# Attention's modulation chunks in two buffers of their own: a two-layer hybrid decoder on one core

## The chip, the core and the metric

The kernel runs on one core of one Trainium2 chip. The metric is the device time of one execution in microseconds (us), as the median of several runs. The engines are named as the profile names them: PE (TensorE, matrix products), PEld (its weight loads), DVE (VectorE), ACT (ScalarE), POOL (GpSimd) and SP (SyncE, which issues nearly all the DMAs here).

## The reference

Two layers over 256 tokens of width 1024. Layer 0 mixes tokens with dilated sliding-window attention (three groups of 16 heads), layer 1 with gated linear attention; each is followed by a gated convolutional feed-forward block. Before every block stands an RMS norm whose scale and shift, like the gate of the residual, come from the conditioning vector:

```
for i in range(DEPTH):
    mod = silu(c) @ w_ada[i] + b_ada[i]            # 1024 -> 6 * 1024
    sh1, sc1, g1, sh2, sc2, g2 = split(mod, 6)
    h = rmsnorm(x, norm_mix[i]) * (1 + sc1) + sh1
    y = dilated_mixture(h, ...) if i % 2 == 0 else gla_mixer(h, ...)
    x = x + g1 * y
    h = rmsnorm(x, norm_ffn[i]) * (1 + sc2) + sh2
    x = x + g2 * conv_ffn(h, ...)
return rmsnorm(x, norm_final)
```

All of it is float32. The matrix `w_ada` is 48 MB in all, and serves a single vector.

## The kernel before

**Weights.** A weight piece is loaded by one DMA from SP into a tile `raw` of the pool `wraw` (four buffers of 2048 columns, 1 MB each over the 128 partitions). `split` (L162) then makes two halves of it for products in three passes: ACT copies `raw` to `whi` (L172, rounded), DVE subtracts to get `wlo` (L178, or L184 through `low_part`). `whi` and `wlo` have three buffers each. `mm3` (L196) multiplies hi by hi, hi by lo and lo by hi, all on PE.

**Modulation.** The product with `w_ada` is not done on PE. It comes in 48 chunks of 1 MB, two halves `s` of 1024 columns each. `ada_load` (L129) brings a chunk in, into the same four buffers of `wraw`; `ada_dot` (L136) multiplies a half with the broadcast `c_bc` and sums along the row in one DVE instruction (L140), then ACT adds the bias (L148 or L150). The first eight chunks are used by the start, one for each of eight blocks `kt` of the input. The other forty are taken one by one by `next_ada` (L441): two after the second attention unit, one after each of the three query-key groups of units 2 to 7 (20 in attention in all), the rest later. In a unit from 2 on, the dot products of a chunk are put behind the group's last evacuation on DVE (`behind(evacuate(...))`, L590); the load of the chunk is not, since `behind` orders only instructions of the same engine as the one named. The two chunks of unit 1 (L606) are behind nothing. In this text the chunks of attention are called c0, c1, c2 and so on; c0 and c1 are those of unit 1.

**Start.** For each `kt` there is a modulation chunk and a weight piece `w0[kt]` (1920 columns), both in `wraw`. The order of the start on DVE and ACT is written out by hand: two dots, the scaling of `x`, a half of `wlo`, `hlo`, the other half of `wlo`. PE multiplies the piece for units 0 and 1 at once (L571, L575).

**Attention.** Eight units (pairs of heads). A unit needs three query-key pieces `wqk` and two value pieces `wv`; a unit's scores and softmax (`attend`, L449) run beside the next unit's projections. Its tiles lie in the pool `att`, which ends with the output projection (`project`, L629). The last quarter of the output projection's weights goes into two tiles `w30` and `w31` of `att`, 1536 columns each, by `last_out` (L613), so that they don't take a place in `wspl`. No other instruction uses these two places.

**Order.** A list scheduler sets the order of each engine's queue: it runs a model of the machine, and whenever an engine is free it takes, of the instructions whose inputs and buffers are there, the one that is earliest in the program. `tc.issue_after` and `behind` add an edge that keeps an instruction behind another on its engine. The bias loads of attention, for example, are kept behind the last load of the start in this way:

```
with tc.issue_after(last_load[0].ins):
    bias = load_bias(u)
```

`shift(pool, columns)` puts an unused tile in a pool, to move what follows it.

Of the kernel before, what the change touches and what calls it, by code (L numbers as in the profile page):

```python
# [11 lines left out]
F32 = mybir.dt.float32  # L12
EXP_LN = "natural_log_exp_and_others"
F32R = mybir.dt.float32r
# [4 lines left out]
P = 128  # L19
D = 1024  # L20
# [37 lines left out]
def trunk(ctx: ExitStack, tc: tile.TileContext, I, out):  # L58
    nc = tc.nc
# [12 lines left out]
    def bank(name="ps", tag=None):  # L72
        tag = tag or next(cycle)
        return psum.tile([P, 512], F32, tag=tag, name=name, bufs={"p": 2, "s": 3, "t": 3}[tag])
# [24 lines left out]
    def col(at):  # L99
        return small[:, at : at + 1]  # L100
# [25 lines left out]

    mod = {}

    def ada_load(l, n, dmas=1):  # L129
        raw = wraw.tile([P, 2048], F32, tag="raw", name="ada_raw")  # L130
        for i in range(dmas):
            c = slice(2048 * i // dmas, 2048 * (i + 1) // dmas)
            nc.sync.dma_start(raw[:, c], I["w_ada"][l, n][:, c])
        return raw

    def ada_dot(l, n, s, raw):  # L136
        piece, kt = ADA_ORDER[2 * n + s]
        dot = tmp.tile([P, 1], F32, tag="dot", name="dot", bufs=4)
        w = raw[:, D * s : D * s + D]
        i = nc.vector.tensor_tensor_reduce(  # L140
            w, w, c_bc, op0=ALU.mult, op1=ALU.add, scale=1.0, scalar=0.0, accum_out=dot,
        )
        m = state.tile([P, 1], F32, tag=f"mod{l}{piece}{kt}", name="mod")
        b = col(C_BADA + 48 * l + 8 * piece + kt)
        if piece in (1, 4):
            g = col((C_NMIX if piece == 1 else C_NFFN) + 8 * l + kt)
            b1 = (16 if piece == 4 else 0) + 8 * l + kt
            j = nc.scalar.activation(m, dot, AF.Identity, scale=g, bias=one_b[:, b1 : b1 + 1])  # L148
        else:
            j = nc.scalar.activation(m, dot, AF.Identity, bias=b)  # L150
        mod[l, piece, kt] = m
        return i, j

    def ada_chunk(l, n):
        raw = ada_load(l, n)
        for s in range(2):
            ada_dot(l, n, s, raw)
# [4 lines left out]
    def split(src, n, dmas=1, after=((), ()), late=(), low=(), lows=True):  # L162
        raw = wraw.tile([P, 2048], F32, tag="raw", name="raw")
        for i in range(dmas):
            c = slice(n * i // dmas, n * (i + 1) // dmas)
            last_load[0] = nc.sync.dma_start(raw[:, c], src[:, c])
        hi = wspl.tile([P, 2048], F32R, tag="whi", name="whi")
        lo = wspl.tile([P, 2048], F32R, tag="wlo", name="wlo")
        for i in range(0, n, n // 2):
            c = slice(i, i + n // 2)  # L170
            with behind(*after[i > 0]):
                copied[0] = nc.scalar.copy(hi[:, c], raw[:, c])  # L172
        if not lows:
            return hi, lo, raw, n // 2
        for i in range(0, n, n // 2):
            c = slice(i, i + n // 2)
            with behind(*(late if i else low)):
                last_lo[0] = nc.vector.tensor_tensor(lo[:, c], raw[:, c], hi[:, c].bitcast(F32), op=ALU.subtract)  # L178
        return hi, lo
# [16 lines left out]
    def mm3(ps, a, b, start, stop):  # L196


        mm(ps, a[0], b[0], start=start, stop=False)  # L199
        mm(ps, a[0], b[1], start=False, stop=False)  # L200
        return mm(ps, a[1], b[0], start=False, stop=stop)  # L201
# [39 lines left out]
    def shift(pool, columns):  # L241

        pad = pool.tile([P, columns], F32, tag=f"pad{len(pads)}", name="pad")
        pads.append(pad)
# [25 lines left out]
    @contextmanager  # L270
    def behind(*those):

        with ExitStack() as st:
            for i in those:
                st.enter_context(tc.issue_after(i.ins))
            yield
# [28 lines left out]
    def shift_columns(l, sub):  # L305
        with behind(*chain[7]):
            for kt in range(KT):
                nc.scalar.copy(early_x[kt][:, T : T + 1], mod[l, 3 * sub, kt])
# [4 lines left out]
    def scale(l, sub, kt):  # L313
        i = nc.scalar.mul(early_x[kt][:, 0:T], x[kt], mod[l, 3 * sub + 1, kt][:, 0:1])
        if kt == 5:
            sixth[:1] = [i]

    def load_early(src):
        early = wraw.tile([P, 2048], F32, tag="raw", name="raw")
        nc.sync.dma_start(early[:, 0 : KT * P], src[:, 0 : KT * P])  # L320
        return early
# [24 lines left out]
    def residual(l, sub, kt, ps):  # L346
        g = mod[l, 3 * sub + 2, kt]
        with behind(*(last_sum if kt == 7 or (l, sub, kt) == (0, 0, 6) else ())):
            i = last_x[kt // 7] = nc.vector.scalar_tensor_tensor(x[kt], ps, g[:, 0:1], x[kt], op0=ALU.mult, op1=ALU.add)
        if kt < 6:  # L350
            squared[1] = i

    def parts(w, at, n=P):
        return w[0][:, at : at + n], w[1][:, at : at + n]
# [5 lines left out]
    att = at_pool.__enter__()  # L360
# [72 lines left out]
    with tc.issue_after(last_load[0].ins):  # L433
        nc.sync.dma_start(x_all, I["xT"])
        nc.sync.dma_start(rows_d, rows)
        nc.sync.dma_start(small[:, C_CW:], I["small"][:, C_CW:])

    o_hi, o_lo = [], []
    rest = [(0, n) for n in range(8, 24)] + [(1, n) for n in range(24)]

    def next_ada():  # L441
        if rest:
            ada_chunk(*rest.pop(0))
# [104 lines left out]
    for u in range(NPAIR):  # L548
# [10 lines left out]
        if u == 0:  # L559
# [5 lines left out]
            for kt in range(KT):  # L565
                s, e = kt == 0, kt == KT - 1

                for a, b in ((0, 0), (1, 0), (0, 1)):
                    for i in range(2 * NG):
                        w = parts(w0[kt], P * i)  # L570
# [10 lines left out]
        else:  # L581
            for g in range(NG):
                w = split(I["wqk"][u - 2, g], 2048)
                pqk = bank("pqk", "p")
                pq, pk = pqk[:, :T], pqk[:, T:]
                for kt in range(KT):
                    s, e = kt == 0, kt == KT - 1
# [4 lines left out]
        if u > 0:  # L592
            pv = [bank("pv", "p") for _ in range(2)]
            for half in range(2):
                with behind(*chain[7]):
                    w = split(I["wv"][u - 1, half], 1536)
# [11 lines left out]
                next_ada()  # L608
    o = list(zip(o_hi, o_lo))

    KO = 6

    def last_out(src):  # L613


        raw = wraw.tile([P, 2048], F32, tag="raw", name="raw")
        nc.sync.dma_start(raw, src)
        n = 2 * P * KO
        own = [att.tile([P, n], F32R, tag=f"w3{s}", name=("whi", "wlo")[s], bufs=1)[:, :] for s in range(2)]
        split_into([(raw[:, i : i + n // 2], own[0][:, i : i + n // 2], own[1][:, i : i + n // 2]) for i in (0, n // 2)],  # L620
                   exps[-1:], (norms[-2:-1], turned[-3:-2]))
        rest = [wspl.tile([P, 2048], F32R, tag=("whi", "wlo")[s], name=("whi", "wlo")[s])[:, :] for s in range(2)]
        split_into([(raw[:, n:], rest[0][:, 0 : 2048 - n], rest[1][:, 0 : 2048 - n])])
        shared[:] = [y[:, 2048 - n :] for y in rest]
        return lambda kt, i: parts(own, 2 * P * kt + P * i) if kt < KO else parts(rest, 2 * P * (kt - KO) + P * i)

    shared = []

    def project(src, o, l, sub):  # L629

        ends = []
        shift_columns(l, 1)
        for n in range(4):
            if l == 0 and n == 3:
                tile_of = last_out(src[n])
            else:

                w = split(src[n], 2048, **(dict(after=(evacuated[:1], ()), low=evacuated[1:]) if n == l == 0 else {}))
                tile_of = lambda kt, i, w=w: parts(w, 2 * P * kt + P * i)
            ps = [bank("py", "ppst"[n])] * 2  # L640
            if n == 3:
                ps[1] = bank("py", "s")
            order = [(kt, i) for kt in range(KT) for i in range(2)]
            if n == 3:
                order.sort(key=lambda x: x[1])
            for kt, i in order:

                first = {(2, 2): last_t, (2, 4): last_po, (2, 5): ends[:1], (3, 0): ends[2:]} if l == 0 else {(2, 2): ends[:1]}
                with behind(*first.get((n, kt), ())):
                    e = mm3(ps[i][:, T * i : T * i + T], tile_of(kt, i), o[kt],  # L650
                            kt == 0 and (n == 3 or i == 0), kt == KT - 1 and (n == 3 or i == 1))
            ends.append(e)
            if n == 3:
                early = load_early(I["w_up"][l, 0])
            for i in range(2):
                residual(l, sub, 2 * n + i, ps[i][:, T * i : T * i + T])
                squared_now = add_square(2 * n + i, alone=(l, n, i) == (0, 3, 0))
                if (l, n) != (0, 3):
                    scale(l, 1, 2 * n + i)
            if (l, n) == (0, 3):  # L660

                with behind(squared_now):
                    for i in range(2):
                        scale(l, 1, 2 * n + i)
        return early

    shift(att, 8)
    early = project(I["w_out_a"], o, 0, 0)
    at_pool.__exit__(None, None, None)


# [169 lines left out]
    for n in range(4):  # L841
        with behind(*((), chain[5], chain[7], glr_copy)[n]):
            w = split(I["w_v_b"][n], 2048) if n else w_first
# [309 lines left out]
```

## Time and profile before

| what | value |
|---|---|
| median of 3 runs | 783.05 us (782.6 to 783.72) |
| the profiled execution's own time | 784.99 us |
| its span, first to last instruction | 783.2 us |
| PE busy | 770.9 us (98%) |
| DVE busy | 643.2 us (82%) |
| ACT busy | 479.9 us (61%) |
| moved by DMA | 184.72 MB, mean 236 GB/s |
| granted PE clock | 0.998 |

The span is shorter than the execution's own time by 1.8 us, which lie before the first and after the last instruction. In the rows a matrix product's end is modelled, so that a busy PE is not a PE at its peak. Start takes the first 54 us or so, attention and its output projection run to about 297 us, the first feed-forward block to about 476 us, the second layer takes the rest.

### The profile page before, as it was taken

The page shows a single profiled execution, that of the slowest core. Times are in us where ns is not written, and L with a number is a line of the kernel's source. Part 1 is how long each engine was busy: PE and PEld are TensorE (multiplying, and loading weights), DVE is VectorE, ACT ScalarE, POOL GpSimd, SP SyncE. Part 2 cuts the span into 40 slices and gives each one's busy share as a digit, 9 for nine tenths or more (in the row PEclk, how much of TensorE's full clock was granted, in tenths as well). Part 3 has the DMA queues.
Part 4 walks back from the last instruction along what each step waited for, and adds up shares of the span by engine and source line. Part 5 has one row for each costly group of instructions (what it writes and reads, how often), then busy time and mean ns, then how long its engine had stood idle before and what let it go on. Part 6 is the DMA issues. An engine that isn't in the chain of part 4 may idle for free.

```text
span 783.2 us, 15925 instructions
## 1 busy us (share of the span) xinstructions
PE 770.9 (98%) x6430; PEld 743.2 (95%) x6430; DVE 643.2 (82%) x1160; ACT 479.9 (61%) x937; POOL 13.9 (2%) x40
## 2 busy tenths in 40 slices
PE   8999999999999999999999999999999999999997
PEld 6999999999999999999999998898999999999997
DVE  6999988879778858999998877797567898899662
ACT  5476565555555657876766646655667866667552
POOL 1000000000000000000000100000010000000000
PEclk9999999999999999999999999999999999999999
DMA  9999677596784736776645984965445665555651
GB/s 349 397 338 363 211 290 286 180 328 203 255 299 164 282 128 232 267 264 228 245 166 195 323 310 177 360 227 203 141 146 186 236 215 179 199 197 196 211 205 54
DMA packets 32616, 184.72 MB, mean 236 GB/s; under 512 B 5852, under 2 KB 7388, under 8 KB 16286
## 3 DMA queue, kind: packets, MB, share of 16 engines
q1 hardware_dynamic: 32160, 183.26, 65.8%
q8 instruction: 50, 0.82, 0.4%
q10 hardware_dynamic: 382, 0.45, 0.2%
q14 instruction: 24, 0.20, 0.1%
HBM read 182.59 MB, written 1.10 MB: 235 GB/s over the span
## 4 chain that ended last, share of the span: by engine, by line
PE 84%; DVE 6%; DMA 6%; ACT 2%; issue 1%; ACTq 0%; DVEq 0%
PE pab L199 10%; PE pab L200 10%; PE pab L201 10%; PE pqk L199 4%; PE pqk L200 4%; PE pqk L201 4%; PE pv L199 4%; PE pv L200 4%; PE pv L201 3%; PE pd L201 3%; PE pd L199 3%; PE pd L200 3%; DVE wlo L178 3%; PE pqk L571 2%; PE py L199 2%; PE py L200 2%
## 5 line engine op out<-in xcount | busy, mean ns | idle before, releaser
L172 ACT CAST whi<-raw 128x1024 fp32r<-128x1024 f32 (+4 forms) x270 | 243.0, 946 | 127.8 <-PE pab L200 40.1
L178 DVE TENSOR_TENSOR wlo<-raw,whi 128x1024 fp32r<-128x1024 f32 (+3 forms) x254 | 270.2, 1093 | 52.2 <-ACT whi L172 51.4
L201 PE MATMUL pab<-hhi,wlo 128*128 128x256 f32 x672 | 184.7, 276 | 0.0
L200 PE MATMUL pab<-hlo,whi 128*128 128x256 f32 x672 | 184.7, 276 | 0.0
L199 PE MATMUL pab<-hhi,whi 128*128 128x256 f32 x672 | 183.2, 277 | 0.0
L140 DVE CUSTOM_DVE_ANT_0 ada_raw<-ada_raw,c_bc 128x1024 f32<-128x1024 f32 x96 | 113.5, 1218 | 16.7 <-DMA ada_raw<-in_w_ada 16.7
L200 PEld LDWEIGHTS pab<-hlo,whi 128*128 128x128 f32 x672 | 126.0, 188 | 0.2
L201 PEld LDWEIGHTS pab<-hhi,wlo 128*128 128x128 f32 x672 | 126.1, 188 | 0.0
L199 PEld LDWEIGHTS pab<-hhi,whi 128*128 128x128 f32 x672 | 125.1, 188 | 0.1
L199 PE MATMUL pqk<-hhi,whi 128*128 128x256 f32 x392 | 109.2, 283 | 0.0
L200 PE MATMUL pqk<-hlo,whi 128*128 128x256 f32 x392 | 108.4, 281 | 0.0
L201 PE MATMUL pqk<-hhi,wlo 128*128 128x256 f32 x392 | 107.8, 282 | 0.0
L201 PE MATMUL pd<-ghi,wlo 128*128 128x256 f32 x352 | 97.2, 276 | 0.5 <-DVE wlo L178 0.5
L200 PE MATMUL pd<-glo,whi 128*128 128x256 f32 x352 | 97.1, 276 | 0.0
L199 PE MATMUL pd<-ghi,whi 128*128 128x256 f32 x352 | 96.8, 276 | 0.0
L199 PEld LDWEIGHTS pqk<-hhi,whi 128*128 128x128 f32 x392 | 73.4, 188 | 0.7
L200 PEld LDWEIGHTS pqk<-hlo,whi 128*128 128x128 f32 x392 | 73.3, 188 | 0.3
L201 PEld LDWEIGHTS pqk<-hhi,wlo 128*128 128x128 f32 x392 | 72.7, 188 | 0.9 <-issue 0.7
L201 PEld LDWEIGHTS pd<-ghi,wlo 128*128 128x128 f32 x352 | 66.1, 188 | 0.7 <-DVE wlo L178 0.7
L200 PEld LDWEIGHTS pd<-glo,whi 128*128 128x128 f32 x352 | 66.1, 188 | 0.0
L199 PEld LDWEIGHTS pd<-ghi,whi 128*128 128x128 f32 x352 | 65.9, 188 | 0.0
L725 ACT ACTIVATE r<-pab,small 128x256 f32<-128x256 f32 x86 | 46.7, 559 | 15.5 <-DVE r L728 15.4
(216 smaller groups left out, 1369.5 us busy)
## 6 DMA issues: line engine op xcount, KB each, us to landing
ada_raw<-in_w_ada SPq DMA_DIRECT2D x47, 1024.0 KB, 6.4
raw<-in_w_up SPq DMA_DIRECT2D x42, 1024.0 KB, 4.9
raw<-in_w_down SPq DMA_DIRECT2D x32, 704.0 KB, 5.5
raw<-in_wqk SPq DMA_DIRECT2D x18, 1024.0 KB, 6.9
raw<-in_wv SPq DMA_DIRECT2D x14, 768.0 KB, 4.7
raw<-in_w SPq DMA_DIRECT2D x7, 960.0 KB, 6.1
raw<-in_w_out_a SPq DMA_DIRECT2D x4, 1024.0 KB, 6.3
raw<-in_w_v_b SPq DMA_DIRECT2D x4, 1024.0 KB, 7.3
```

Source lines behind the costliest of these rows:

```text
L140: i = nc.vector.tensor_tensor_reduce(w, w, c_bc, op0=ALU.mult, op1=ALU.add, scale=1.0, scalar=0.0, accum_out=dot,)
L172: copied[0] = nc.scalar.copy(hi[:, c], raw[:, c])
L178: last_lo[0] = nc.vector.tensor_tensor(lo[:, c], raw[:, c], hi[:, c].bitcast(F32), op=ALU.subtract)
L199: mm(ps, a[0], b[0], start=start, stop=False)
L200: mm(ps, a[0], b[1], start=False, stop=False)
L201: return mm(ps, a[1], b[0], start=False, stop=stop)
L571: mm(pqk[i], w[a], h[kt][b], start=s and i % 2 == 0 and (a, b) == (0, 0), stop=e and i % 2 == 1 and b == 1)
L725: nc.scalar.activation(r, u[:, :T], AF.Identity, scale=cw[2], bias=col(C_CB + 44 * l + f))
```

## The change

From the end of the start's loop to the end of the output projection's `project`, `ada_load` no longer takes a buffer of `wraw`. It takes the two places `w30` and `w31` of `att`, one for each half `s`, 1024 of their 1536 columns, and loads the halves with two DMAs of 512 KB. Each place has one buffer, so that a half's load waits until the dot of the chunk before has read that half. In attention the four buffers of `wraw` hold weights alone. The two places are now declared ahead of the other tiles of `att`, with an unused tile of 56 columns ahead of them and one of 8 behind them; the 8 columns ahead of `project` are gone. After attention all is as it was.

```diff
+    places = []
+
     def ada_load(l, n, dmas=1):
+        if places:
+
+            raw = [places[0].tile([P, D], F32, tag=f"w3{s}", name="ada_raw", bufs=1)[:, :] for s in range(2)]
+            for s in range(2):
+                nc.sync.dma_start(raw[s], I["w_ada"][l, n][:, D * s : D * s + D])
+            return raw
         raw = wraw.tile([P, 2048], F32, tag="raw", name="ada_raw")
         for i in range(dmas):
             c = slice(2048 * i // dmas, 2048 * (i + 1) // dmas)
             nc.sync.dma_start(raw[:, c], I["w_ada"][l, n][:, c])
-        return raw
+        return [raw[:, D * s : D * s + D] for s in range(2)]
 
     def ada_dot(l, n, s, raw):
...
-        w = raw[:, D * s : D * s + D]
+        w = raw[s]
...
+    KO = 6
     o_hi, o_lo = [], []
     rest = [(0, n) for n in range(8, 24)] + [(1, n) for n in range(24)]
+
+
+    shift(att, 56)
+    for s in range(2):
+        att.tile([P, 2 * P * KO], F32R, tag=f"w3{s}", name="w3", bufs=1)
+    shift(att, 8)
+    places.append(att)
...
-    KO = 6
-
     def last_out(src):
...
-    shift(att, 8)
     early = project(I["w_out_a"], o, 0, 0)
+    places.clear()
     at_pool.__exit__(None, None, None)
```

## The prediction

> **What bounds the kernel now.** I read the page first, then the busy time by stretch, then who waited for whom on PE in attention, then the chain of waits at the one stall found there, and last the timelines of SP, DVE, ACT and POOL in the start.
>
> ```profile
> span 783.2 us, 15925 instructions
> PE 770.9 (98%) x6430; PEld 743.2 (95%) x6430; DVE 643.2 (82%) x1160; ACT 479.9 (61%) x937; POOL 13.9 (2%) x40
> ```
>
> PE is busy in all but 12.3 us of the span. A change that touches only loads and buffers can win no more than PE's idle time in the stretch that it touches, but it can lose without such a limit. So the question is how much PE idles in attention. The next rows are stretches of time: length, then busy us (and instructions) of PE, PEld, DVE, ACT and POOL, then granted clock, DMA share and GB/s.
>
> ```profile
> 8.00:14.00 6.00, 5.95 (x24) 3.90 (x24) 4.67 (x8) 4.76 (x9) 0.00 (x0) 1.00 1.03 417
> 14.00:30.00 16.00, 16.00 (x131) 16.00 (x130) 15.88 (x26) 9.02 (x19) 0.00 (x0) 1.00 1.01 415
> 30.00:46.00 16.00, 16.00 (x130) 16.00 (x129) 15.83 (x25) 8.16 (x15) 0.00 (x0) 1.00 1.00 377
> 46.00:54.00 8.00, 8.00 (x67) 8.00 (x67) 7.57 (x12) 5.49 (x9) 0.00 (x0) 1.00 0.97 326
> ...
> 158.00:190.00 32.00, 32.00 (x278) 30.59 (x277) 26.09 (x52) 17.78 (x41) 0.20 (x2) 1.00 0.72 253
> 222.00:254.00 32.00, 31.17 (x270) 29.88 (x269) 24.95 (x49) 17.67 (x39) 0.00 (x0) 1.00 0.68 247
> ```
>
> Two things are to be seen. In attention (158 on) PE is full, DVE has some 6 us of 32 free, and DMA is at 0.7. In the start (8 to 54) three things are full at once: PE, DVE (15.88 of 16) and DMA (1.01 and 1.00 of its engines). Whatever is added to the start is paid there; in attention it is mostly hidden. PE's waits from 54 to 292 us are these (total, times, longest):
>
> ```profile
> PE po L503 <- ACT mod L150: 0.8, 1, 0.8
> PE pv L199 <- ACT v L543: 0.2, 1, 0.2
> ```
>
> and the chain at the larger one:
>
> ```profile
> 243.82 5.55 DMA raw<-in_wv
> ...
> 249.45 1.57 ACT whi L172 x2
> 251.02 0.28 ACT mod L148
> 251.31 0.36 ACT pt L499
> ...
> 251.89 1.08 PE po L503 x8
> ```
>
> ACT stood before the cast of a value piece that landed late; the copy of the turned probabilities was queued behind it, and PE waited for that. A late weight is just what the change is about, so it may well remove this one. The whole prize in attention is 0.8 + 0.2 = 1.0 us.
>
> **The change part by part: weights in attention.** Weights do wait now for chunks and land late:
>
> ```profile
> SPq L166 <- DVE dot L140: 25.9, 6, 5.8
> ...
> ACT whi L172 <- DMA raw<-in_wv: 28.0, 11, 4.3
> ACT whi L172 <- DMA raw<-in_wqk: 17.1, 9, 2.3
> ```
>
> The first row is SP held at a weight's issue by a dot; the other two are ACT idle until a weight lands, 45.1 us in 20 waits. With four buffers for weights alone I expect most of both to go. But ACT is not the bound: of 45.1 us only the 1.0 us above reached PE. What is late next is nothing; PE itself. Worth: between 0 and -1.0 us; I take -1.0, since the chain above shows the DMA as the root of the larger.
>
> **Chunks in attention.** Each half now has one place, so a load can go only when the dot before it is done, and the next dot can come only when that load has landed. Twenty chunks become forty DMAs and SP issues one more for each (some 0.33 us on a queue that mostly waits).
>
> ```profile
> ada_raw<-in_w_ada SPq DMA_DIRECT2D x47, 1024.0 KB, 6.4
> raw<-in_w SPq DMA_DIRECT2D x7, 960.0 KB, 6.1
> raw<-in_w_up SPq DMA_DIRECT2D x4, 512.0 KB, 3.7
> ```
>
> A half's round is then about 3.7 us (512 KB) to 6.4 us (two halves together, as 1 MB) plus 1.22 us for the dot, 5 to 7.6 us. A unit of 32 us has three chunks, 10.7 us each on average, so the rounds fit; where two groups of a unit stand closer together than that, a dot comes a few us later. Queued behind a late dot on DVE are the next `wlo` and the softmax steps, for which PE waits in the end. DVE's 6 us free in a unit stand against that. I take 0, with 0 to +3 us as bounds (at most half a microsecond for each of the six units of three chunks).
>
> In the start loads of about 1 MB take 6.1 to 6.4 us each from issue to landing, yet 415 GB/s flow, which is one every 2.5 us: what a DMA takes beside its bytes is hidden behind its neighbours. The Trainium skill has a rule against this part: DMA: Bandwidth & Descriptors (sections on the anatomy of one DMA and on bandwidth) wants DMAs of 1 MiB and more, and puts a fixed cost of about 2 us on each. By that, twenty more DMAs would be 40 us of queue time, if none overlapped; the trace says that they do.
>
> **The start: what is let loose.** This is the part that decides. Before, a chunk of attention had to wait for a buffer of `wraw`, and the start's loads, earlier in the program, took these first. Now c0 needs only `w30` and `w31`, which nothing has used, and no edge holds it back (the bias loads have one, the chunks have none). What the scheduler does with such an instruction can be seen on POOL and SP:
>
> ```profile
> 0.87 1.45 POOL L547 MEMSET q<- 128x512 f32 x3
> 3.05 0.20 POOL L554 MEMSET k<- 128x4 f32 x4
> ...
> 6.82 0.49 SPq L166 DMA_DIRECT2D raw<-in_w  x1
> 11.93 0.33 SPq L133 DMA_DIRECT2D ada_raw<-in_w_ada  x1
> 15.87 0.33 SPq L166 DMA_DIRECT2D raw<-in_w  x1
> ...
> 55.79 3.28 SPq L133 DMA_DIRECT2D ada_raw<-in_w_ada  x2
> ```
>
> The memsets of attention's tiles, written behind the whole start (L547, L554), run in the first 3.3 us, because POOL was free and their tiles too. SP is free from 7.3 to 11.9 us, with all four buffers taken. So c0, which went at 55.79, should go there now, ahead of the start's third chunk and weight piece.
>
> Its price: 1 MB at 415 GB/s is 2.5 us of a queue without a gap. The cover is the time by which a piece lands ahead of its use. Weight pieces are issued at 15.87 and land 6.1 us later, at about 22.0; the cast starts at 22.78:
>
> ```profile
> 22.78 0.98 ACT L172 CAST whi<-raw 128x960 fp32r<-128x960 f32 x1
> ```
>
> so 0.8 us are covered and 1.7 us are not. The Trainium skill (DMA: Bandwidth & Descriptors, section on bandwidth) puts a core's limit at HBM at about 358 GB/s; by that the 1 MB would be 2.9 us. The 415 and 417 GB/s of the rows above are over that limit and decide.
>
> Next come c0's dots. They stand last in the program's order, but DVE has a hole in each `kt`:
>
> ```profile
> 26.59 1.22 DVE L140 CUSTOM_DVE_ANT_0 ada_raw<-ada_raw,c_bc 128x1024 f32<-128x1024 f32 x1
> ...
> 30.35 0.48 DVE L287 SCALAR_TENSOR_TENSOR hlo<-xr,mod,hhi 128x256 fp32r<-128x256 f32 x1
> 30.88 1.16 DVE L184 TENSOR_TENSOR wlo<-raw,whi 128x960 fp32r<-128x960 f32 x1
> 31.96 1.22 DVE L140 CUSTOM_DVE_ANT_0 ada_raw<-ada_raw,c_bc 128x1024 f32<-128x1024 f32 x1
> ...
> 51.08 1.15 DVE L184 TENSOR_TENSOR wlo<-raw,whi 128x960 fp32r<-128x960 f32 x1
> ```
>
> From 30.83 to 30.88 DVE waits for `whi`. A scheduler that takes whatever is ready puts a dot of c0 there if its model has the hole as well, and holes get larger once loads are late. Each such dot costs 1.14 us (the step from one dot to the next) on an engine whose round, 31.96 - 26.59 = 5.37 us, is as long as PE's:
>
> ```profile
> 41.54 1.41 PE pqk L571 x12
> ...
> 46.83 2.12 PE pqk L571 x18
> ...
> 52.12 1.90 PE pqk L571 x16
> ```
>
> (52.12 - 46.83 = 5.29). And with c0's dots done, c1's load goes, then c1's dots and c2's load; c2's dots are held by their evacuation. So up to three chunks, 3 x 2.5 = 7.5 us of the queue, and four dots, 4 x 1.14 = 4.6 us of DVE, move into the start. That DVE and DMA have less to do after the start is no gain, since PE's only waits there are the two shown.
>
> The sum for that case. Queue: c0 and c1 ahead of the last weight pieces, 5.0 us; less 0.8 us of cover; less what the queue can catch up from 30 to 46, where it moved 377 of 415 GB/s, 16 x (1 - 377/415) = 1.5 us: 2.7 us. DVE: 4.6 us. The dots fall into holes that the late loads make, so the two overlap: between 2.7 and 4.6, and I take the middle, 3.7. PE has some cover at the end of the start: the `wlo` of the last `kt` ends at 52.23, and is needed after six products, 0.7 us into the group that starts at 52.12: 0.6 us. So PE ends the start 3.1 us later, and has nothing else to do meanwhile, since units 0 and 1 need all eight blocks. From 54 us on PE is the bound and carries this to the end. With attention's -1.0: +2.1 us. The profiled execution would go from 784.99 to 787.1, and the median, 1.9 us below it before, from 783.05 to 785.2.
>
> **Tiles that move.** The other tiles of `att` go up by 2 x 6144 + 4 x 64 = 12,544 bytes, an even number of 256-byte steps, and `w30` and `w31` go down; durations should stay. I cost this at nothing; were a pattern of addresses to change PE's step in attention by 1%, it would be 2.4 us of 240 either way.
>
> **The rivals.**
> 1. *Only c0's load comes forward* (no hole in the model's DVE, dots after the start). Then 1.7 - 0.6 = 1.1 us are lost in the start and 1.0 won: 783.2, between 782.6 and 784.4. For it: the holes are 0.05 us small. Against: they come in every `kt`.
> 2. *Faster: the start keeps its order and attention sheds its stalls.* It decides if c0 goes after the start's loads, or if its 2.5 us are covered after all. Then -1.0 us is sure, and a little more comes if weights that are ready in time let PE change its kind of product less often. A change costs about 0.1 us (the first product behind scores takes longer than the next):
>
> ```profile
> 233.93 0.38 PE L199 MATMUL pqk<-hhi,whi 128*128 128x256 f32 x1
> 234.15 0.28 PE L200 MATMUL pqk<-hlo,whi 128*128 128x256 f32 x1
> ```
>
> Ten fewer give 783.05 - 1.0 - 1.0 = 781.0. Against it are POOL's memsets.
> 3. *Slower in attention.* DVE stands before dots whose single place was filled late: up to +3 us less the 1.0, 785.0, with an undisturbed start.
> 4. *The change doesn't do what it says*: the weights can't run ahead, since `whi` and `wlo` keep three buffers. Then attention's 1.0 us stays: 783.05, or 786.2 with the start's loss.
>
> **How the numbers follow.** Forecast 0.45 (slower, with the fourth rival's second half in it), first rival 0.24, second 0.20, third 0.07, fourth without a loss 0.04. A measurement of this kernel can tell about 0.2%, 1.6 us, from no change. The forecast and the third are slower (0.52); the first and fourth are the same (0.28), as is the part of the second that wins the stalls alone, 782.05 (0.04), which leaves 0.16 for faster. The range goes from 781.4, into the second rival, to 787.6, where all three chunks delay the start (7.5 - 0.8 - 1.5 - 0.6 = 4.6 us) and attention wins nothing. The forecast's own range is 784.0 to 787.6.
>
> **What would show it.** Right: two loads `ada_raw` of 512 KB on SP before 12 us, dots of attention among those of the start, PE's rounds longer than 5.29 us between 15 and 60, and the output projection starting 2 us later. Wrong: c0 issued after 43 us and the start's rounds unchanged; or the loads early and the rounds unchanged, which would mean that the queue's full share hid some slack. In attention the rows of ACT waiting for `in_wv` should shrink from 28.0 us to a few; if they don't, the weights don't run ahead.

## The result: 1.5% slower, and the profile after

The changed kernel takes 795.31 us (median of 4 runs, 794.41 to 797.4), against 783.38 us (782.6 to 784.85) for the kernel before, run beside it. The ratio is 1.0152, with a 95% interval of 1.0126 to 1.0178. The profiled execution takes 794.95 us, with a span of 793.2 us, 10.0 us more than before. The forecast was 785.2 us, at most 787.6: the direction was right, the size was not.

The head of the page of the changed kernel, and then two of the prediction's stretches (length, busy us and instructions of PE, PEld, DVE, ACT and POOL, granted clock, DMA share, GB/s):

```profile
span 793.2 us, 15987 instructions
PE 773.6 (98%) x6430; PEld 743.5 (94%) x6430; DVE 645.9 (81%) x1160; ACT 482.0 (61%) x937; POOL 13.8 (2%) x40
...
14.00:30.00 16.00, 14.27 (x113) 14.06 (x112) 13.17 (x22) 6.54 (x13) 0.00 (x0) 1.00 1.02 417
...
222.00:254.00 32.00, 30.40 (x258) 28.51 (x258) 23.88 (x48) 14.92 (x33) 0.00 (x0) 1.00 0.70 222
```

PE, DVE and ACT are each busy 2 to 3 us longer. What has changed most is the idle time of PE: 1.73 us from 14 to 30 us, where there was none, and 1.60 us from 222 to 254 us, where there was 0.83. PE's waits from 8 to 300 us, in the changed kernel:

```profile
PE s L476 <- ACT k L548: 5.6, 4, 1.6
PE pqk L587 <- ACT hhi L293: 3.9, 2, 2.2
PE t L514 <- DVE pn L509: 0.6, 1, 0.6
PE pv L207 <- ACT v L559: 0.3, 1, 0.3
```

Of the two rows that the prediction quoted, the 0.8 us behind `mod` is gone and the 0.2 us is still there. The first three rows are new. To split the 10.0 us I use two marks that all kernels have, the first product `pv` (start done) and the first product `early` (attention done). The kernel before:

```profile
57.62 0.45 PE L199 MATMUL pv<-whi,hhi 128*128 128x384 f32 x1 [0.25 <-ACT v L543]
293.14 0.38 PE L329 MATMUL early<-early_x,raw 128*128 128x257 f32 x1
```

and the changed one:

```profile
61.81 0.45 PE L207 MATMUL pv<-whi,hhi 128*128 128x384 f32 x1 [0.25 <-ACT v L559]
304.94 0.38 PE L337 MATMUL early<-early_x,raw 128*128 128x257 f32 x1
```

The start ends 4.19 us later. Attention takes 243.13 us, before 235.52: 7.61 us more. From `early` to the end of the span it is 488.26 us, before 490.06, which makes up the sum of 10.0. I don't count that last difference to the change: among the kernels below this stretch takes 487.2 to 492.7 us (x8_none and x2_layout), though their edits all bear on what lies ahead of it.

**The start.** SP's queue, and DVE in front of a chunk:

```profile
6.73 0.63 SPq L174 DMA_DIRECT2D raw<-in_w  x1
8.18 0.80 SPq L136 DMA_DIRECT2D ada_raw<-in_w_ada  x2
11.24 0.33 SPq L141 DMA_DIRECT2D ada_raw<-in_w_ada  x1
15.19 0.33 SPq L174 DMA_DIRECT2D raw<-in_w  x1
```

```profile
21.90 1.23 DVE L148 CUSTOM_DVE_ANT_0 ada_raw<-ada_raw,c_bc 128x1024 f32<-128x1024 f32 x1 [1.14 <-DMA ada_raw<-in_w_ada]
...
50.28 1.22 DVE L148 CUSTOM_DVE_ANT_0 ada_raw<-ada_raw,c_bc 128x1024 f32<-128x1024 f32 x1
...
51.43 1.22 DVE L148 CUSTOM_DVE_ANT_0 ada_raw<-ada_raw,c_bc 128x1024 f32<-128x1024 f32 x1
...
52.57 1.22 DVE L148 CUSTOM_DVE_ANT_0 ada_raw<-ada_raw,c_bc 128x1024 f32<-128x1024 f32 x1
...
53.72 1.22 DVE L148 CUSTOM_DVE_ANT_0 ada_raw<-ada_raw,c_bc 128x1024 f32<-128x1024 f32 x1
```

The two halves of c0 are issued at 8.18 us, in the idle time that the prediction named. At the end of the start four dots stand in a row, where the last `kt` has two: c0's stand among them, and c1's load goes only at 58.22 us, behind the start. PE waits after each place:

```profile
26.69 0.97 PE L587 MATMUL pqk<-hhi,whi 128*128 128x256 f32 x6 [1.73 <-ACT hhi L293]
...
56.00 0.74 PE L587 MATMUL pqk<-hhi,whi 128*128 128x256 f32 x4 [2.16 <-ACT hhi L293]
```

**Attention.** ACT's casts of weights from 150 to 250 us, before and after (busy us, mean ns | idle time just before them, and what ended it):

```profile
L172 ACT CAST whi<-raw 128x1024 fp32r<-128x1024 f32 (+1 forms) x31 | 28.2, 957 | 30.7 <-DMA raw<-in_wv 20.0 <-DMA raw<-in_wqk 8.6 <-PE s L467 2.2
```

```profile
L180 ACT CAST whi<-raw 128x1024 fp32r<-128x1024 f32 (+1 forms) x30 | 27.0, 956 | 3.3 <-issue 3.3
```

The change does what it says: ACT no longer waits for weights. Its timeline in the changed kernel at one of the stalls of 1.6 us shows what ACT does instead (`q` and `k` at L543 and L548 are its steps of the evacuation of the unit's first query-key group):

```profile
184.91 1.56 ACT L180 CAST whi<-raw 128x768 fp32r<-128x768 f32 x2
186.49 0.38 ACT L543 ACTIVATE q<-pqk 64x256 fp32r<-64x256 f32 x1
...
188.85 0.38 ACT L543 ACTIVATE q<-pqk 64x256 fp32r<-64x256 f32 x1
190.33 1.56 ACT L180 CAST whi<-raw 128x768 fp32r<-128x768 f32 x2 [1.10 <-issue]
191.92 0.38 ACT L538 ACTIVATE q<-pqk 128x256 f32<-128x256 f32 x1
192.20 0.37 ACT L548 CAST k<-pqk 128x256 fp32r<-128x256 f32 x1
```

DVE's timeline at the same place has the subtractions of the same weights between its own steps (L544, L549), and PE's has the stall:

```profile
186.37 1.82 DVE L186 TENSOR_TENSOR wlo<-raw,whi 128x768 fp32r<-128x768 f32 x2
188.11 0.41 DVE L544 SCALAR_TENSOR_TENSOR q<-pqk,q 64x256 fp32r<-64x256 f32 x1
...
190.32 0.43 DVE L544 SCALAR_TENSOR_TENSOR q<-pqk,q 64x256 fp32r<-64x256 f32 x1
...
191.65 1.83 DVE L186 TENSOR_TENSOR wlo<-raw,whi 128x768 fp32r<-128x768 f32 x2
193.39 0.42 DVE L538 COPY k<-pqk 128x256 f32<-128x256 f32 x1
193.72 0.41 DVE L549 TENSOR_TENSOR k<-pqk,k 128x256 fp32r<-128x256 f32 x1
```

```profile
192.62 0.98 PE L476 MATMUL s<-k,q 128*128 128x256 f32 x6 [1.60 <-ACT k L548]
```

128x768 is the half of a value piece (`wv`). The evacuation is a chain in which ACT and DVE take turns, six steps of about 0.4 us (softmax steps, which the fences leave out, also stand between them). One pair of the value weights' casts runs just ahead of its first step and another inside it, from 190.33 to 191.89, with two pairs of subtractions; the chain takes from 186.49 us to the end of ACT's step `k` at 192.57, 6.1 us, and the scores wait for that `k`. In the kernel before, ACT at the same work:

```profile
209.12 0.38 ACT L527 ACTIVATE q<-pqk 64x256 fp32r<-64x256 f32 x1 [0.26 <-PE pqk L201]
...
211.86 0.38 ACT L527 ACTIVATE q<-pqk 64x256 fp32r<-64x256 f32 x1
213.89 0.37 ACT L532 CAST k<-pqk 128x256 fp32r<-128x256 f32 x1 [1.66 <-DVE q L528]
215.62 1.57 ACT L172 CAST whi<-raw 128x768 fp32r<-128x768 f32 x2 [1.36 <-DMA raw<-in_wv]
```

There the chain takes 5.1 us (209.12 to 214.26), with query-key weights' work of DVE in it, and the value weights land only behind it. Their first half gets a buffer at 211.28, their second at 217.11, when a chunk's dots, which are kept behind that same evacuation, are done.

These are not single cases. In units 2 to 7 of the changed kernel the chain takes 3.5 to 6.7 us, with a pair of value casts just ahead of it in all six, and a second pair inside it in four; just these four have the stall. In the kernel before it takes 2.8 to 5.3 us, and no value cast stands ahead of it or inside. So the waiting that the change removes had kept the value weights out of the chain.

PE's busy time from the first `pv` to the first `early`, before and after, shows how much of the 7.6 us is idle time:

```profile
57.62:293.14 235.52, 234.68 (x2032) 223.06 (x2033) 193.48 (x398) 134.69 (x303) 3.29 (x14) 1.00 0.69 249
```

```profile
61.81:304.94 243.13, 236.99 (x2032) 223.17 (x2033) 193.29 (x397) 135.44 (x301) 3.04 (x14) 1.00 0.69 235
```

Idle time goes from 0.84 to 6.14 us, which is 5.3 us. The other 2.3 us are the same products being busy longer.

### The profile page after: what moved, and what is told of

The parts are those of the page before. It is cut to its first block, busy times and chain, and to the rows that moved or that the text cites. A ratio compares the mean times of both kernels' runs of the same rounds, so it can differ in the third digit from the quotient of the medians.

```text
span 793.2 us, 15987 instructions
## 1 busy us (share of the span) xinstructions
PE 773.6 (98%) x6430; PEld 743.5 (94%) x6430; DVE 645.9 (81%) x1160; ACT 482.0 (61%) x937; POOL 13.8 (2%) x40
## 4 chain that ended last, share of the span: by engine, by line
PE 90%; DVE 4%; ACT 3%; DMA 1%; issue 1%; ACTq 0%; DVEq 0%
PE pab L207 10%; PE pab L208 10%; PE pab L209 10%; PE pqk L207 5%; PE pqk L209 5%; PE pd L209 5%; PE pd L208 5%; PE pqk L208 5%; PE pd L207 5%; PE pv L207 4%; PE pv L208 3%; PE pv L209 3%; PE s L476 2%; PE py L207 2%; PE py L209 2%; PE py L208 2%
```

## The experiments

My theory at this point: two separate losses, c0 in the start and the value weights' casts in the evacuation. Rivals: the moved tiles; chunks that come late to their dots; the number of weight buffers; a late start that upsets attention. "Attention" is the time from the first `pv` to the first `early`; ratios are to the kernel before, run beside each, with their 95% intervals.

**x1_hold: only the start undone.** Unit 1's two chunks are kept behind its last weight load.

```diff
         if u == 1:
-            for n in range(2):
-                next_ada()
+            with tc.issue_after(last_load[0].ins):
+                for n in range(2):
+                    next_ada()
```

> The changed kernel, but the loads of the two chunks of unit 1 (c0, c1) are kept on SP behind unit 1's last value weights, so that none goes during the start. Theory A (the start loses 4.2 us, 1.9 by c0's load in a full DMA queue and 2.3 by c0's two dots on a full DVE; attention loses some 7 us because weights that are early let ACT's casts go ahead of evacuations that PE waits for): about 791.1 us, PE's stalls of 1.9 and 2.3 us before 54 us gone, the ones of 1.76 us in attention still there. Theory B (the single places make the chunks late, DVE stands before their dots, and PE waits for that): the same 791.1 for this run. If both stalls of the start stay, the loads weren't their cause.

798.01 us, 1.0176 (1.0144 to 1.0207), and not the 791.1 that both theories expected. The start is as before (first `pv` at 57.67 us), so its loss is c0's coming forward. But attention takes 248.26 us:

```profile
PE s L476 <- ACT k L548: 7.5, 5, 1.6
PE po L519 <- DVE pt L515: 2.6, 1, 2.6
```

There are now five stalls behind `k`, and one of 2.6 us in unit 2, from 86.2 us. A second pair of value casts now stands inside the chain in all six units. Holding c0 there won nothing in all.

**x2_layout: the tiles' new places alone**, with the chunks still in `wraw`.

```diff
-    places.append(att)
```

> The new places in the pool alone: w30 and w31 are declared early, with the 56 and 8 unused columns, but attention's chunks still come into the four raw buffers. Both theories: as before, 783.4 us within 0.3%. If the moved tiles cost something, it is slower and the same products take longer each (pitch over 113 to 118 ns).

783.1 us, 0.9985 (0.9965 to 1.0005); attention 234.83 us. The moved tiles cost nothing.

**x3_three: three rotating places** of 1024 columns in place of two fixed ones, so that a chunk's loads wait less for dots.

```diff
-            raw = [places[0].tile([P, D], F32, tag=f"w3{s}", name="ada_raw", bufs=1)[:, :] for s in range(2)]
+            raw = [places[0].tile([P, D], F32, tag="w3", name="ada_raw", bufs=3)[:, :] for s in range(2)]
...
-    KO = 6
+    KO = 4
...
```

(`KO` is the number of the output weights' blocks that go into these places: 1024 columns instead of 1536.)

> The changed kernel with three places of 1024 columns that the halves take in turn, in the same 12 KB (the last output weights keep 1024 columns there instead of 1536): a half's load then waits for the dot three halves back, not two. Theory B: DVE's wait for chunks (22.2 us in the changed kernel) falls to a half or less, and attention's loss of 7 us with it: about 788 to 790 us. Theory A: DVE's wait falls, but the total stays at 795 us within 2 us, since the weights are as early as in the changed kernel.

799.27 us, 1.0188 (1.0155 to 1.0221). DVE's wait for chunks in attention, first of the changed kernel, then of this one:

```profile
DVE ada_raw L148 <- DMA ada_raw<-in_w_ada: 21.1, 11, 4.2
```

```profile
DVE ada_raw L148 <- DMA ada_raw<-in_w_ada: 11.9, 4, 4.1
```

9.2 us less of it, and PE's wait behind `k` is 6.4 us, not less than 5.6; attention takes 243.77 us. Late chunks are not the cause. The start got worse, 4.3 us of waits at `hhi`, since a third place lets a further half come forward.

**x4_held, x5_held2: fewer buffers for the weights.** One, or two, of the four raw buffers are held by an unused tile until the last unit.

```diff
     places.append(att)
+    held = [wraw.tile([P, 2048], F32, tag="raw", name="held") for _ in range(2)]
+    for z in held:
+        nc.gpsimd.memset(z[:, 0:1], 0.0)
...
```

(This is x5_held2's edit; the lines that let the buffers go in the last unit are left out.)

> The changed kernel, but one of the four raw buffers is held by an unused tile from the end of the start to unit 7, so that weights have three buffers in attention and chunks their single places. Theory A: weights are less early, casts go later, attention's loss shrinks: 788 to 792 us. Theory B: the chunks are as late as in the changed kernel, and it stays at 795 us or above.

> As x4_held, but two of the four raw buffers are held to unit 7, so that weights have two in attention (before, a chunk sat in a buffer for some 20 us, and weights had a little over two). Theory A, now made precise (casts and subtractions of value weights that are there too early fill the gaps of the six-step evacuation of a unit's first group, so that the scores that wait for its k, and the bank that it holds, come late): PE's wait of scores for k (5.6 us in the changed kernel) goes, and the total comes to about 788 us, with the start's 4.2 us left. Theory C (the prefetch doesn't matter; it is the places' chunks that reorder attention): it stays at 795 to 798 us with the same 1.7 us stalls.

796.12 us, 1.0152 (1.0118 to 1.0187), attention 243.96 us; and 801.45 us, 1.0199 (1.0137 to 1.0261), where the first `pv` comes behind the first scores, so that the mark can't be compared. PE's waits behind `k` are 3.9 and 6.2 us. My theory had expected 788 to 792 and about 788 us; both runs came out nearer to what the rival about the chunks expected, so that these two don't speak for my theory. What they do show is that with two or three buffers a second pair of value casts still stands inside the chain, in six and in four of units 2 to 7. So it is not how many buffers the weights have; that it is the lack of a chunk in front of them rests on the next run.

**x8_none: no chunks in attention.** Loads and dots of its 20 chunks are left out; the modulation columns get another value, so the kernel computes something else there.

```diff
     def ada_chunk(l, n):
+        if places:
+            for s in range(2):
+                piece, kt = ADA_ORDER[2 * n + s]
+                m = state.tile([P, 1], F32, tag=f"mod{l}{piece}{kt}", name="mod")
+                nc.scalar.activation(m, c_bc[:, 0:1], AF.Identity, bias=col(C_BADA + 48 * l + 8 * piece + kt))
+                mod[l, piece, kt] = m
+            return
```

> The changed kernel without attention's 20 chunks: neither their loads nor their dot products run (the modulation columns are made from something else), the rest of the chunks is as in the changed kernel. Weights have the four raw buffers alone. Theory A: the start is as before (0 instead of 4.2 us lost), but the stalls of scores behind k stay, though DVE has 49 us less to do: 787 to 790 us. Theory B or C (late or reordered chunks are the cause): the stalls are gone and it is at 782 us or below.

798.99 us, 1.0171 (1.0101 to 1.0241). The total can't be compared, since the stand-in instructions themselves came forward into the start: PE waits 4.0 us there and then runs at a granted clock of 0.50 from 14 to 18.5 us, and the first `pv` comes at 65.77 us. Attention takes 243.24 us, and this is its wait:

```profile
PE s L483 <- ACT k L555: 6.4, 4, 1.6
```

Without a single chunk the four stalls are all there, 1.60 us each. So neither the chunks' loads nor their dots make attention slower; their absence from `wraw` does.

**x6_evac: the casts kept out of the evacuation.** From unit 2 on, the casts and subtractions of `wv` stand behind ACT's and DVE's last step of the unit's first evacuation. All else is as in the changed kernel.

```diff
-        nc.scalar.copy(kh, pk)
-        return nc.vector.tensor_tensor(kl, pk, kh.bitcast(F32), op=ALU.subtract)
+        first_k[:] = [nc.scalar.copy(kh, pk)]
+        first_k.append(nc.vector.tensor_tensor(kl, pk, kh.bitcast(F32), op=ALU.subtract))
+        return first_k[1]
...
-                    w = split(I["wv"][u - 1, half], 1536)
+                    w = split(I["wv"][u - 1, half], 1536, **(dict(after=(first_k[:1], first_k[:1]), low=first_k[1:], late=first_k[1:]) if u > 1 else {}))
```

> The changed kernel, with the casts and the subtractions of a unit's value weights kept behind the last steps (ACT's and DVE's) of the evacuation of that unit's first query-key group, from unit 2 on. Theory A: the evacuation takes 4 to 6 us again instead of 8 to 10, the stalls of scores behind k go (5.6 us), and the total is 787 to 790 us, the start's 4.2 us being left. Theory C: the stalls go elsewhere and it stays above 793 us.

788.0 us, 1.0049 (1.0022 to 1.0075), 7.3 us under the changed kernel's median. Attention takes 232.99 us, less than before's 235.52, and PE's waits from 54 to 300 us are:

```profile
PE pqk L590 <- ACT hhi L293: 1.2, 1, 1.2
PE py L207 <- ACT v L562: 0.5, 1, 0.5
PE pv L207 <- ACT v L562: 0.3, 1, 0.3
```

The stalls behind `k` are gone with edges of order and nothing else, and in units 3 to 7 the chain takes 3.2 to 3.4 us. This is what shows the cause in attention. Whether the casts on ACT or the subtractions on DVE do more of the harm was not tried apart. What is left is the start.

**y4_unit1: the start's loss alone.** Only unit 1's chunks use the places.

```diff
         if u == 1:
             for n in range(2):
                 next_ada()
+            places.clear()
```

> The changed kernel, but only the two chunks of unit 1 use the two places; from unit 2 on the chunks take raw buffers as in the kernel before. The start is that of the changed kernel (c0's load and its dots come forward), attention that of the kernel before. Theory A (the two losses are separate): first value product at about 61.8 us, 4.2 later than before, attention at about 235.5 us, no wait of scores for k of more than 1 us in all; total 787 to 788. Theory B (the late start is what upsets attention): attention at 240 us or more, total over 791. Rival C (a loss in the start is given back later, as PE has waits to fill): total 783 to 785.

788.27 us, 1.0049 (1.0024 to 1.0075). First `pv` at 61.91 us, attention 235.51 us: to 0.01 us that of the kernel before. One unit has a pair of value casts inside the chain here, without a stall. The start's loss is not given back, and a late start doesn't disturb attention.

**z2_att: attention's loss alone.** Unit 1's chunks are in `wraw`, as before; later chunks use the places, each load behind its own group's weight load.

```diff
             for s in range(2):
-                nc.sync.dma_start(raw[s], I["w_ada"][l, n][:, D * s : D * s + D])
+            with tc.issue_after(last_load[0].ins):
+                for s in range(2):
+                    nc.sync.dma_start(raw[s], I["w_ada"][l, n][:, D * s : D * s + D])
...
         if u == 1:
+            own = places.pop()
             for n in range(2):
                 next_ada()
+            places.append(own)
```

> The changed kernel with the chunks of unit 1 in raw buffers as in the kernel before, and each later chunk's load behind the load of its own group's query-key weights: the start of the kernel before, and from unit 2 on the places as in the changed kernel, with no order on the casts of the value weights. Theory A (attention's loss stands by itself): first value product at 57 to 57.9 us, waits of scores for k of 4 to 6 us in all, attention at 242 to 244 us, total 790 to 791.5. Theory B (attention's loss needs the late start or the early chunk loads): attention 235 to 237, total 783 to 785.

790.85 us, 1.0094 (1.0057 to 1.013). Attention takes 241.63 us, with 4.7 us of waits behind `k` in three stalls. So it stands by itself; the 241.63 us are just under the 242 to 244 that were expected. By medians, each against its own runs of before, y4_unit1 loses 5.0 us and this one 7.5, together 12.5; the whole change loses 11.9. That they nearly add up is in part luck: here the first `pv` came at 60.95 us, 3.3 us later than before (why is told in the last section), and attention lost 6.1 us, not 7.6.

**y3_load: the load without the dots.** x6_evac, with unit 1's chunks in `wraw`. Now c2's load comes forward into the start, but its dots are held by their evacuation.

> x6_evac, but the two chunks of unit 1 take raw buffers as in the kernel before; the places serve from unit 2 on. The load of the next chunk, c2, then comes forward into the start, but its dots are kept behind unit 2's evacuation. So the start pays for the queue alone, without dots. Theory A (two prices, the 1 MB in the queue and the two dots): PE's stall near 24 us stays, 1.5 to 2.4 us, the one near 54 us is gone; first product of the value group at 59.0 to 60.0 us; with attention at about 233 us the total is 783 to 785. Theory B (the start's loss is all from the dots): first value product at 57.6, total 781. Theory C (all from the load, and the later stall only follows from it): first value product at 61.8, total 788.

785.66 us, 1.0035 (1.0008 to 1.0062). First `pv` at 60.00 us, and PE waits once:

```profile
26.94 0.74 PE L590 MATMUL pqk<-hhi,whi 128*128 128x256 f32 x4 [1.44 <-ACT hhi L293]
```

So the start has two prices: 2.4 us for the 1 MB (60.00 less 57.62), and the rest of 4.2 us, 1.8, for the two dots. Attention took 235.45 us here, not the 233 expected.

**y1_order: the order alone**, in the kernel before (x6_evac's edit, chunks in `wraw`).

> The kernel before (chunks in the four raw buffers), with one order added: from the third unit on, the casts and subtractions of the value weights stand behind ACT's and DVE's last step of the unit's first query-key evacuation. It asks whether the order alone is worth what attention gained in x6_evac (232.99 us against 235.52). Theory A (in the kernel before, the chunk in front of the value weights already keeps most of them out of the evacuation, though not all): a gain of 0 to 1.5 us, total about 782.5, and attention at 234 to 235.5 us. Theory B (the gain of x6_evac is all from this order, none from the chunks' own places): attention 233, total about 780.9. Theory C (casts that come late for other reasons are now later still): PE waits for whi, total up to 786.

782.79 us, 0.998 (0.9957 to 1.0003); attention 234.49 us. A gain of 1.0 us in the trace, which the runs can't tell from none. The same edges take 10.1 us from attention in the changed kernel (243.13 to 232.99), so what they repair there is the change's doing.

**x7_both, y6_best, z1_group: versions meant to be faster than both.** x7_both is x6_evac with x1_hold's edge. y6_best is y3_load with all loads into the places behind the start's last load. z1_group is y3_load with each chunk's load behind its own group's weight, that is z2_att with x6_evac's order.

> x6_evac and x1_hold together: chunks c0 and c1 behind unit 1's last value weights, and value weights behind the first evacuation. Theory A: both losses gone, 782 to 785 us, level with before or up to 1 us better. Theory C, or if holding the loads disturbs the first units as in x1_hold: 787 us or more.

> x6_evac with both ways into the start closed: the two chunks of unit 1 take raw buffers as in the kernel before, and the loads into the places are kept behind the last load of the start. Theory A (start and evacuation are the change's only two losses): first value product at 57.4 to 57.9 us as before, attention at 233 us as in x6_evac, the second layer some 1 to 2 us better than before as in the changed kernel; total 779.5 to 781.5, under both kernels. Rival B (whatever order is held in the first units shows up later, as in x7_both, whose attention took 237.44 us): attention 235 to 238, total 783 to 786. Rival C (a third loss that the other two hid): over 786.

> x6_evac with the chunks of unit 1 in raw buffers as in the kernel before, and each later chunk's load kept on SP's queue behind the load of its own group's query-key weights, so that none comes forward. Start and first units then have the loads in the order of the kernel before. Theory A (start and evacuation are the change's only losses, and the weights' four buffers are worth a little): pqk to first value product 42.7 us as before, attention from there 233.0 to 234.5 us (before 235.52), total 780.5 to 782.5. Rival B (the 2.5 us that x6_evac gained in attention came from its late start, the first units finding their weights ready): attention 235 to 236, total 782.5 to 784. Rival C (the places cost something that is not seen yet): attention 237 or more, total over 785.

x7_both: 786.19 us, 1.0032 (1.0002 to 1.0061), attention 237.44 us, between its two expectations. y6_best: 786.27 us, 1.0034 (1.0011 to 1.0056); none of its three expectations was met. Its first `pv` came at 59.70 us, with c2's load, issued at 43.96, ahead of the first value weights; PE also waited 1.4 us for a `whi` and 1.6 us for a `wlo`, at 74 and 77 us; attention took 234.27. (The profiled execution, 783.21 us, is the fastest of its twelve.) z1_group: 782.9 us, 1.0005 (0.9977 to 1.0033), first `pv` at 57.67 us, attention 234.34 us. PE from 150 to 250 us, in the changed kernel and in z1_group:

```profile
150.00:250.00 100.00, 95.21 (x805) 89.50 (x804) 76.69 (x151) 52.77 (x116) 0.41 (x4) 1.00 0.71 233
```

```profile
150.00:250.00 100.00, 100.00 (x871) 95.66 (x870) 83.53 (x167) 57.72 (x128) 0.40 (x4) 1.00 0.71 247
```

With both losses removed the chunks' own places win nothing that the runs can tell. z1_group (234.34 us) and y1_order (234.49 us) have the same attention with and without them. The 232.99 us of x6_evac were not reached with an undisturbed start; that they came from its late start was not tried by itself. No version beats the kernel before beyond its interval.

## Why the prediction was wrong

**Right: what bounds the kernel, and where the change could lose.** PE was full in attention, so the change could win 1 us there and lose without a limit. That was written down, but the forecast used the limit only for the gain.

**Right: c0 comes forward, and what its load costs.** Issued at 8.18 us, in the idle time from 7.3 to 11.9; 1.7 us were reckoned, PE's wait is 1.73 us, and by the end of the start 2.4 us in y3_load. That the wait agrees to 0.03 us is luck: behind the same 1 MB it is 1.44 us in y3_load and 2.26 us in x6_evac. The sign named for attention came true too: ACT's waits for `in_wv` went from 28.0 to 0.4 us.

**Partly wrong: the rest of the start's sum.** Up to three chunks and four dots were to come forward, and load and dots were to overlap, 3.1 us in all. One chunk came, with two dots, and the two prices did not overlap: they lie 30 us apart (1.73 and 2.16 us of waits) and add, to 4.2 us at the end of the start. The dots didn't fall into the holes that the late load made, but in front of the last block's, where nothing follows to hide them. The term was a quarter too small.

**Wrong: "What is late next is nothing; PE itself".** This is the step that failed. It priced weights in attention at -1.0 to 0 us and chunks at 0 to +3; the measured +7.6 lies outside both. The prediction followed each wait that goes to the engine that had been waiting, found ACT off the bound, and stopped. It didn't ask what ACT would do in the time set free. ACT and DVE are off the bound on average, but for some 5 us in each unit they carry the evacuation, for which PE waits at its end; that chain was not looked at. The row "ACT whi <- DMA raw<-in_wv: 28.0" was read as waste, and it was what kept casts out of the chain.

**How much of the 7.6 us is named.** Four stalls behind `k` are 5.6 us, and one of 0.6 us before `t` is new; the 0.8 us behind `mod` are gone. Together that is the 5.3 us of idle time. The other 2.3 us are PE's busy time for the same products (236.99 against 234.68 us), which I can't put down to one row. All of it went with the order of x6_evac, where idle time is 0.52 us and busy time 232.47; why that is below the kernel before stays open.

**The rivals.** The first (only c0's load) had the right chunk, without its dots. The second was wrong, though attention can lose its stalls (x6_evac). The third's mechanism is in the trace (DVE waits 21.1 us for chunks), but x3_three and x8_none show that PE doesn't pay for it. The fourth was wrong: three buffers of `whi` and `wlo` do let weights run ahead. None of the four had attention lose more than 3 us. One slip had no effect: 12,544 bytes are 49 steps of 256, not an even number, and x2_layout shows that the move costs nothing.

## What to carry to other kernels

A wait on an engine that is not the bound can be what keeps that engine free for a short chain that the bound does wait for. Before taking such a wait away, look for what becomes ready earlier, in which gaps a scheduler will put it, and whether a chain of turns between two engines stands there; if so, hold the new work behind the chain's last step. And when a transfer gets a place of its own, every edge that its old buffer gave for free, in the start too, has to be written down again.

## What the runs showed of the hardware

In the kernel before, twelve warm-up products take 1.36 us from 13.52 us on, 0.11 us each, and eight from 6.69 us on take 1.86 us, 0.23 us each: PE runs at half its rate up to about 12 us. In the profiled executions of z2_att and y4_unit1 it did so until about 19 us. The first six products of the start, in the kernel before and in z2_att:

```profile
14.88 0.94 PE L571 MATMUL pqk<-hhi,whi 128*128 128x256 f32 x6
```

```profile
17.33 1.63 PE L588 MATMUL pqk<-hhi,whi 128*128 128x256 f32 x6
```

The same six take 1.63 us, as against 0.94, and come 2.45 us later, behind warm-up products that take longer too, although the granted clock of the stretch from 11 to 18.5 us is listed as 1.00 in y4_unit1:

```profile
11.00:18.50 7.50, 7.50 (x29) 5.32 (x28) 6.66 (x12) 5.66 (x14) 0.00 (x0) 1.00 1.02 417
```

29 instructions stand there, 53 before. Up to 12.1 us PE's rows in z2_att and in the kernel before begin within 0.02 us of each other, so that what PE had done by then doesn't explain the difference. The Trainium skill (TensorE: Matmul & The Clock Gate, Part 1) says that PE's clock starts at half and is let up at the end of a window that runs freely, so that the number of slow products differs from run to run of one kernel. The half rate agrees with these traces, whose clock column doesn't show it (in x8_none it does, with 0.50 from 14 to 18.5 us); that one kernel differs from run to run, and why the half rate lasted some 7 us longer in these two, no run here shows. The half rate explains z2_att's late first `pv`, and in y4_unit1 it hid: PE was late anyway, the wait near 26 us is missing, and the start ends at 61.91 us, as in the changed kernel.
